# A hybrid decoder layer: every matmul operand starts at a multiple of 128 bytes in SBUF

## The chip, the core and the metric

The kernel runs on one core of one Trainium2 chip. The metric is the device time of one execution in microseconds; the median of three runs is taken. TensorE is written PE (matmuls) and PEld (weight loads), VectorE DVE, ScalarE ACT, GpSimd POOL, SyncE SP.

## What is computed

One decoder layer on a sequence of 256 rows of width 1024, all float32. Cut to what matters here:

```python
h = x @ W_in                                   # split into qA kA vA zA qB kB vB zB gA gB
yA = (swa_sink_attention(qA, kA, vA) * silu(zA)) @ W_oA
yB = (moba_attention(qB, kB, vB) * silu(zB)) @ W_oB
m  = sigmoid(gA + bA) * yA + sigmoid(gB + bB) * yB
x_new = layer_norm(alpha * x + m @ W_out, gamma, beta)
```

## The kernel before

Every large product is made three times, so that float32 accuracy is reached with the type float32r. A weight tile comes by DMA into `raw` (128 x 1024). ACT writes a rounded copy `wh` (line 137, for the last matrix line 134), DVE the rest `wl` = `raw` - `wh` (lines 152 and 149). The activations have such halves too: `xh`, `xl` (the input), `yh`, `yl` (the gated attention), `mh`, `ml` (the merged branches, both in the tile `mm`). A product is then `wh`*`xh` + `wh`*`xl` + `wl`*`xh`.

`contract` (lines 176 to 183) does that for one output tile of 128 columns: lines 180 and 181 alternate over the eight (or four) pieces of the contraction, line 183 follows with `wl`. Each matmul has a new stationary operand, 128 x 128 out of `wh` or `wl`, and a moving operand of 256 columns out of `xh`, `xl`, `yh` or `yl`. There are 37 such tiles of 24 matmuls over the input (`project`), and 16 of 12 matmuls over `yh` and `yl`: 1080 matmuls of 256 columns.

The stages, in order of time: the values (line 292, 320 columns wide, the weights are the moving operand); 21 projections with the attention of eight head pairs among them (scores lines 220 to 222, transposes line 257, values lines 274 and 276); the two gates (16 projections, each followed by 12 matmuls of the output projection of its branch); the last product with `w_out` (line 399), where `mm` is stationary and the weight tiles `wh`, `wl` move.

The last product is done for two row halves. In the first (`t == 0`) two accumulators of 512 columns run together. In the second the columns are taken in three passes: 512 columns, then the third quarter with two columns more (258), then the fourth quarter (256). The two columns more hold the row sums of the fourth quarter of `w_out` (`sums`, put there by POOL in `place_sums`), so that the mean of the whole row is known before the last pass is done, and only the last quarter's normalising is left behind it. For that each of the 16 tiles `wh` and `wl` has four quarters of 258 columns (`OW = 258`).

The order of all instructions is the order of the code; the pools only give addresses. `wh` and `wl` have eight buffers each. A tile of 4 x 258 float32 has 4128 bytes, 32 more than a multiple of 128, so that neighbouring buffers start 32 bytes further round in a line of 128. The small tiles (8, 16 or 32 bytes for a partition) lie among the large ones in the same pools and shift what follows.

Of the kernel before, what the change touches and what calls it, by code (L numbers as in the profile page):

```python
# [11 lines left out]
F32 = mybir.dt.float32  # L12
F32R = mybir.dt.float32r
BF16 = mybir.dt.bfloat16
AF = mybir.ActivationFunctionType
ALU = mybir.AluOpType
# [21 lines left out]
WARM = 9  # L38
RAWS = 5

OW = 258

E = 192

# [2 lines left out]
def hybrid_layer(ctx: ExitStack, tc: tile.TileContext, xT, x2, w_t, w_v, w_a, w_b, w_o,  # L47
# [2 lines left out]
    const = ctx.enter_context(tc.tile_pool(name="const", bufs=1))  # L50
    wp = ctx.enter_context(tc.tile_pool(name="wp", bufs=1))
    work = ctx.enter_context(tc.tile_pool(name="work", bufs=2))
    psum = ctx.enter_context(tc.tile_pool(name="psum", bufs=1, space=bass.MemoryType.PSUM))
    dram = ctx.enter_context(tc.tile_pool(name="dram", bufs=1, space=bass.MemoryType.DRAM))
    ctx.enter_context(tc.manual_schedule())
# [15 lines left out]
    oh = work.tile([NB, RL], F32, tag="res", name="oh")  # L71
    nc.gpsimd.dma_start(tab, table)
    nc.gpsimd.dma_start(oh, onehot)
    sink = const.tile([P, 8], F32, name="sink")
    nc.gpsimd.dma_start(sink, sinks)
    bg = const.tile([P, 16], F32, name="bg")
    nc.gpsimd.dma_start(bg, b_gate)
    ident = const.tile([P, P], F32, name="ident")
    make_identity(nc, ident)
    nsink = const.tile([P, 8], F32, name="nsink")  # L80
    eps = const.tile([P, 1], F32, name="eps")
    nc.gpsimd.memset(eps, LN_EPS)


# [19 lines left out]
    order += [("o", k) for k in range(NK)]  # L104
    ahead = {"v": 2, "t": 3, "a": 4, "b": 5, "o": 7}
    raws, ready = {}, {}
    sums = const.tile([P, NK], F32, name="sums")

    def quarters(w):
        return w.rearrange("p (a b) -> p a b", a=4)[:, :, :S]  # L110

    def fetch(kind, n):

        if kind == "r":

            for a in (2 * n, 2 * n + 1):
                src = bass.AP(tensor=rd.tensor, offset=rd.offset + (a // 8) * 16 * RW + (a % 8) * RL,
                              ap=[[RW + 8, 16], [1, 8], [1, S]])
                nc.sync.dma_start(toep[:, a, :], src)  # L119
            return  # L120
        if kind == "v":
            nc.sync.dma_start(xraw[:, n, :], xT[:, n, :])
            nc.scalar.activation(xh[:, n, :], xraw[:, n, :], AF.Copy)
        width = 640 if kind == "v" else 1024
        src = {"v": lambda: w_v[:, n, :], "t": lambda: w_t[n], "a": lambda: w_a[n], "b": lambda: w_b[n],
               "o": lambda: w_o[n * P:(n + 1) * P, :]}[kind]()
        raw = wp.tile([P, 1024], F32, tag="raw", name="wraw", bufs=RAWS)
        wh = wp.tile([P, 4 * OW], F32R, tag="wh", name="wh", bufs=8)
        parts = 2 if (kind, n) == ("v", 0) else 1
        cuts = [slice(i * width // parts, (i + 1) * width // parts) for i in range(parts)]  # L130
        for cut in cuts:
            nc.sync.dma_start(raw[:, cut], src[:, cut])  # L132
        if kind == "o":
            nc.scalar.activation(quarters(wh), raw.rearrange("p (a b) -> p a b", a=4), AF.Copy)  # L134
        else:
            for cut in cuts:
                nc.scalar.activation(wh[:, cut], raw[:, cut], AF.Copy)  # L137
        raws[kind, n] = raw, wh, width

    def split(kind, n):  # L140

        if kind == "r":
            return
        if kind == "v":
            nc.vector.tensor_sub(xl[:, n, :], xraw[:, n, :], xh[:, n, :].bitcast(F32))
        raw, wh, width = raws.pop((kind, n))
        wl = wp.tile([P, 4 * OW], F32R, tag="wl", name="wl", bufs=8)
        if kind == "o":
            nc.vector.tensor_sub(quarters(wl), raw.rearrange("p (a b) -> p a b", a=4), quarters(wh).bitcast(F32))  # L149
            nc.vector.tensor_reduce(sums[:, n:n + 1], raw[:, 3 * S:], axis=mybir.AxisListType.X, op=ALU.add)  # L150
        else:
            nc.vector.tensor_sub(wl[:, :width], raw[:, :width], wh[:, :width].bitcast(F32))  # L152
        ready[kind, n] = wh, wl

    cursors = [0, 0]
# [16 lines left out]
    def weights(kind, n):  # L172
        lead(kind, n)
        return ready[kind, n]
# [33 lines left out]
    def scores(q, b, heads, sinks_at):  # L208
# [1 line left out]
        qh, ql = q  # L210
        kh, kl = kbd[b]
        pr = work.tile([P, 2, RL], F32, name="pr_", bufs=4)
        nm = work.tile([P, 4], F32, name="nm", bufs=3)
        sm = work.tile([P, 4], F32, name="sm", bufs=3)
        outs = []
        for blk in range(2):
            n = P * (blk + 1)
# [13 lines left out]
                outs.append((dst, at))  # L231
        es = None
        if sinks_at is not None:
            es = work.tile([P, 4], F32, name="es", bufs=3)
            sk = sink[:, sinks_at:sinks_at + 2].unsqueeze(1).to_broadcast([P, 2, 2])
            nc.vector.tensor_tensor(es.rearrange("p (a b) -> p a b", a=2), nm.rearrange("p (a b) -> p a b", a=2), sk,
                                    op=ALU.add)
            nc.scalar.activation(es, es, AF.Exp)
        return pr, outs, sm, es

    def normalise(pr, outs, sm, es):
        if es is not None:
            nc.vector.tensor_add(sm, sm, es)
        rs = work.tile([P, 4], F32, name="rs")
        nc.vector.reciprocal(rs, sm)
        first = pr[:, :, :P]
        nc.gpsimd.tensor_tensor(first, first, rs[:, :2].unsqueeze(2).to_broadcast([P, 2, P]), op=ALU.mult)
        for dst, at in outs[2:]:
            nc.vector.tensor_scalar_mul(dst, dst, rs[:, at:at + 1])
# [120 lines left out]
    gb = const.tile([P, 2, D], F32, tag="ov8", name="gb")  # L370
    nc.sync.dma_start(gb[:, 0, :], gamma.to_broadcast([P, D]))
    nc.sync.dma_start(gb[:, 1, :], beta.to_broadcast([P, D]))
    sd = work.tile([P, 1], F32, name="sd")
    nc.scalar.activation(sd, eps, AF.Sqrt)

    xs = work.tile([P, 1], F32, name="xs")
    nc.vector.tensor_reduce(xs, xr[:, 1, 3 * S:], axis=mybir.AxisListType.X, op=ALU.add)
    nc.vector.tensor_scalar_mul(xs, xs, -ALPHA / D)

    def place_sums():  # L380

        parts = [work.tile([P, NK], F32R, name=f"sums_{i}", bufs=1) for i in range(2)]
        nc.scalar.activation(parts[0], sums, AF.Copy)  # L383
        nc.vector.tensor_sub(parts[1], sums, parts[0].bitcast(F32))
        for k in range(NK):
            for w, part in zip(ready["o", k], parts):
                nc.gpsimd.tensor_copy(w[:, 2 * OW + S:3 * OW], part[:, k:k + 1].to_broadcast([P, 2]))  # L387

    for t in range(2):
        ts = slice(t * P, (t + 1) * P)  # L390
        res = work.tile([P, D], F32, tag="res", name="res")
        st = work.tile([P, 4, 6], F32, name="st")

        def products(accs):
            for k in range(NK):
                wh, wl = (w.rearrange("p (a b) -> p a b", a=4) for w in weights("o", k))
                for a, w, s0, s1 in ((mh, wh, k == 0, False), (ml, wh, False, False), (mh, wl, False, k == NK - 1)):
                    for acc, q, n, cols in accs:
                        nc.tensor.matmul(acc, a[:, k, ts], w[:, q:q + n, :cols], start=s0, stop=s1)  # L399
            if t == 0:  # L400
                place_sums()
            for acc, q, n, _ in accs:
                cut = slice(q * S, (q + n) * S)
                nc.vector.scalar_tensor_tensor(res[:, cut], xr[:, t, cut], ALPHA, acc[:, :n * S], op0=ALU.mult, op1=ALU.add)
                for i in range(q, q + n):
                    nc.vector.bn_stats(st[:, i, :], res[:, i * S:(i + 1) * S])

        def centre(cut, below):
            nc.vector.scalar_tensor_tensor(res[:, cut], res[:, cut], below, gb[:, 0, cut], op0=ALU.add, op1=ALU.mult)
# [3 lines left out]
            nc.gpsimd.tensor_tensor(res[:, early], res[:, early], gb[:, 0, early], op=ALU.mult)  # L413

        early = slice(0, E)
        mv = work.tile([P, 2], F32, name="mv")
        below = work.tile([P, 1], F32, name="below")
        sd = work.tile([P, 1], F32, name="sd")
        rstd = work.tile([P, 1], F32, name="rstd")
        if t == 0:  # L420
            products([(bank("acc"), 0, 2, S), (bank("acc"), 2, 2, S)])
            nc.vector.bn_aggr(mv, st)
            nc.scalar.activation(sd, mv[:, 1:2], AF.Sqrt, bias=eps)
            nc.vector.tensor_scalar_mul(below, mv[:, 0:1], -1.0)
            centre_early(below)
            centre(slice(E, D), below)
        else:
            products([(bank("sc"), 0, 2, S)])
            acc = bank("sc")[:, :OW]
            products([(acc, 2, 1, OW)])  # L430

            part = work.tile([P, 2], F32, name="part")
            nc.vector.bn_aggr(part, st[:, :3, :])
            nc.vector.scalar_tensor_tensor(below, acc[:, S:S + 1], -1.0 / D, xs, op0=ALU.mult, op1=ALU.add)
            nc.vector.scalar_tensor_tensor(below, part[:, 0:1], -0.75, below, op0=ALU.mult, op1=ALU.add)
            centre_early(below)
            centre(slice(E, 3 * S), below)
            products([(bank("pt")[:, :S], 3, 1, S)])
            nc.vector.bn_aggr(mv, st)
            nc.scalar.activation(sd, mv[:, 1:2], AF.Sqrt, bias=eps)  # L440
            centre(slice(3 * S, D), below)
        nc.vector.reciprocal(rstd, sd)

        nc.scalar.activation(res[:, early], res[:, early], AF.Copy, scale=rstd)
# [76 lines left out]
```

## Time and profile before

| | us |
|---|---|
| median of 3 runs | 201.25 |
| lowest, highest | 200.58, 202.72 |
| the profiled execution | 200.9 |
| its span, first to last instruction | 199.1 |

The profiled execution's own time is 1.8 us over its span. The profile gives a matmul's start as measured, its end as modelled; a matmul's row is longer than its share of PE's time, since matmuls overlap. What one costs in a stream is therefore read from start to start here, or from the chain of waits, whose rows hold no overlap.

### The profile page before, as it was taken

To read this page: it belongs to the slowest core of one execution; us is meant where nothing else is said; L and a number is where in the kernel's file an instruction comes from. 1 tells how busy PE (TensorE), PEld (TensorE's weight loads), DVE (VectorE), ACT (ScalarE), POOL (GpSimd) and SP (SyncE) were. 2 spreads that over 40 slices of the span, in tenths; PEclk is the share of its full clock that TensorE was granted. 3 is DMA by queue.
4 is the path that set the end of the run, shared out by engine and by line. 5 is a ranking of instruction groups with operands and counts; after the bars stand their busy time and mean duration, and the time that the engine had idled before them with its cause. 6 is when DMAs were issued, how large, how long until landed. Compare 5 with 4: busy or idle time off the path is not lost.

```text
span 199.1 us, 3871 instructions
## 1 busy us (share of the span) xinstructions
PE 190.9 (96%) x1469; PEld 179.2 (90%) x1469; DVE 137.9 (69%) x280; ACT 114.5 (58%) x228; POOL 19.0 (10%) x45
## 2 busy tenths in 40 slices
PE   8999999999999999999999999999999999999960
PEld 2899999899998998999999999999999999888960
DVE  0686368999987875586768537446585878786773
ACT  5585658677985776765679454246554746630110
POOL 7160000110110101100000000000000000012311
PEclk9999999999999999999999999999999999999995
DMA  5999999947354333044656774573847499300202
GB/s 143 314 402 343 256 298 302 284 137 237 135 163 156 107 105 110 0 154 165 209 185 239 288 243 137 182 216 135 291 145 249 166 304 359 148 0 0 105 0 105
DMA packets 14081, 37.42 MB, mean 188 GB/s; under 512 B 1632, under 2 KB 5744, under 8 KB 14064
## 3 DMA queue, kind: packets, MB, share of 16 engines
q1 hardware_dynamic: 13520, 36.51, 56.2%
q0 software_dynamic: 256, 0.49, 0.7%
q8 instruction: 11, 0.18, 0.3%
q10 hardware_dynamic: 288, 0.20, 0.3%
q14 instruction: 6, 0.05, 0.1%
HBM read 35.75 MB, written 1.44 MB: 187 GB/s over the span
## 4 chain that ended last, share of the span: by engine, by line
PE 77%; DMA 9%; SPq 4%; DVE 3%; ACT 2%; issue 1%; DVEq 0%; ACTq 0%
PE ps_acc L180 19%; PE ps_acc L181 19%; PE ps_acc L183 19%; PE ps_acc L399 6%; PE ps_sc L399 4%; DMA wraw<-in_w_t 4%; PE ps_pt L257 3%; DMA rd<-rvec 3%; DMA wraw<-in_w_v 3%; PE ps_o L274 2%; SPq L119 2%; SPq L132 1%; PE ps_pt L399 1%; PE ps_sc L220 1%; ACT wh L137 1%; PE ps_sc L221 1%
## 5 line engine op out<-in xcount | busy, mean ns | idle before, releaser
L180 PE MATMUL ps_acc<-xh,wh 128*128 128x256 f32 x296 | 71.6, 281 | 0.0
L181 PE MATMUL ps_acc<-xl,wh 128*128 128x256 f32 x296 | 71.3, 280 | 0.0
L152 DVE TENSOR_TENSOR wl<-wraw,wh 128x1024 fp32r<-128x1024 f32 (+1 forms) x53 | 60.7, 1161 | 5.7 <-ACT wh L137 5.4
L137 ACT ACTIVATE wh<-wraw 128x1024 fp32r<-128x1024 f32 (+2 forms) x54 | 52.8, 991 | 8.6 <-DMA wraw<-in_w_t 5.2
L180 PEld LDWEIGHTS ps_acc<-xh,wh 128*128 128x128 f32 x296 | 55.8, 189 | 0.5 <-issue 0.2
L181 PEld LDWEIGHTS ps_acc<-xl,wh 128*128 128x128 f32 x296 | 55.7, 188 | 0.4
L183 PE MATMUL ps_acc<-xh,wl 128*128 128x256 f32 x296 | 40.9, 280 | 0.0
L183 PEld LDWEIGHTS ps_acc<-xh,wl 128*128 128x128 f32 x296 | 37.5, 188 | 0.0
L354 ACT ACTIVATE sg<-ps_acc,bg 128x256 f32<-128x256 f32 x16 | 7.6, 476 | 19.3 <-PE ps_acc L183 19.2
L180 PE MATMUL ps_acc<-yh,wh 128*128 128x256 f32 x64 | 15.8, 281 | 0.0
L181 PE MATMUL ps_acc<-yl,wh 128*128 128x256 f32 x64 | 15.8, 280 | 0.0
L359 DVE TENSOR_TENSOR ga<-ps_acc,sg 128x256 f32<-128x256 f32 x8 | 3.4, 425 | 13.9 <-ACT wh L137 13.9
L180 PEld LDWEIGHTS ps_acc<-yh,wh 128*128 128x128 f32 x64 | 12.1, 188 | 0.0
L181 PEld LDWEIGHTS ps_acc<-yl,wh 128*128 128x128 f32 x64 | 12.0, 188 | 0.0
L387 POOL CAST wh<-sums 128x2 fp32r<-128x2 f32 x8 | 1.5, 187 | 93.8 <-ACT sums L383 93.8
L183 PE MATMUL ps_acc<-yh,wl 128*128 128x256 f32 x64 | 10.1, 279 | 0.0
L364 ACT ACTIVATE mm<-m 128x256 fp32r<-128x256 f32 x8 | 3.4, 419 | 11.6 <-DVE m L363 11.6
L149 DVE TENSOR_TENSOR wl<-wraw,wh 128x1024 fp32r<-128x1024 f32 x8 | 9.8, 1220 | 0.1
L399 PE MATMUL ps_acc<-wh,mm 128*128 128x512 f32 x32 | 8.8, 396 | 0.0
L183 PEld LDWEIGHTS ps_acc<-yh,wl 128*128 128x128 f32 x64 | 8.6, 188 | 0.0
L134 ACT ACTIVATE wh<-wraw 128x1024 fp32r<-128x1024 f32 x8 | 8.2, 1049 | 0.0
L399 PE MATMUL ps_sc<-wh,mm 128*128 128x512 f32 (+1 forms) x32 | 7.9, 339 | 0.0
(162 smaller groups left out, 288.0 us busy)
## 6 DMA issues: line engine op xcount, KB each, us to landing
wraw<-in_w_t SPq DMA_DIRECT2D x37, 512.0 KB, 3.6
wraw<-in_w_o SPq DMA_DIRECT2D x8, 512.0 KB, 5.1
wraw<-in_w_v SPq DMA_DIRECT2D x7, 320.0 KB, 5.4
toep<-rd SPq DMA_DIRECT2D x16, 128.0 KB, 7.1
wraw<-in_w_a SPq DMA_DIRECT2D x4, 512.0 KB, 3.6
wraw<-in_w_b SPq DMA_DIRECT2D x4, 512.0 KB, 3.9
xraw<-in_xT SPq DMA_DIRECT2D x8, 128.0 KB, 5.2
xr<-in_x SPq DMA_DIRECT2D x1, 1024.0 KB, 7.8
```

The costliest lines, as they stand in the source:

```text
L119: nc.sync.dma_start(toep[:, a, :], src)
L134: nc.scalar.activation(quarters(wh), raw.rearrange("p (a b) -> p a b", a=4), AF.Copy)
L137: nc.scalar.activation(wh[:, cut], raw[:, cut], AF.Copy)
L149: nc.vector.tensor_sub(quarters(wl), raw.rearrange("p (a b) -> p a b", a=4), quarters(wh).bitcast(F32))
L152: nc.vector.tensor_sub(wl[:, :width], raw[:, :width], wh[:, :width].bitcast(F32))
L180: nc.tensor.matmul(acc, wh[:, cols[k]], ah[:, a0 + k, :], start=(k == 0), stop=False)
L181: nc.tensor.matmul(acc, wh[:, cols[k]], al[:, a0 + k, :], start=False, stop=False)
L183: nc.tensor.matmul(acc, wl[:, cols[k]], ah[:, a0 + k, :], start=False, stop=(k == n - 1))
L257: nc.tensor.transpose(pt[:, b * P:(b + 1) * P], pr[:, j, b * P:(b + 1) * P], ident)
L274: nc.tensor.matmul(o[r, :], vv[:, 0, c], pts[:, :S], start=True, stop=False)
L354: nc.scalar.activation(sg, acc, AF.Sigmoid, bias=bg[:, at:at + 1])
L399: nc.tensor.matmul(acc, a[:, k, ts], w[:, q:q + n, :cols], start=s0, stop=s1)
```

## The change

The tiles that are smaller than a line of 128 bytes go to a pool of their own, `small`, which is opened after the three others and lies behind them. `OW` becomes 1056: a weight tile is one row of 1056 columns, 4224 bytes, 33 times 128. The quarters are no longer apart. The two columns of sums stand behind the fourth quarter (columns 1024 and 1025); they hold the row sums of the third quarter now, the second pass of the second row half takes the fourth quarter and the two columns (`[3 * S : D + 2]`), and the last pass takes the third quarter. Everything that went by quarters (`quarters`, the reshaped weights, the statistics' order) is adapted to it. Since the columns that are normalised early are now two pieces, one DVE instruction of 576 columns becomes two, of 320 and of 256.

Where the tiles start, in bytes of a partition modulo 128, as the built programs place them:

| tile | before | after |
|---|---|---|
| `xh`, `xl`, `xraw`, `kall`, `pts` | 32 | 0 |
| `yh`, `yl`, `mm`, `vv`, `qh`, `ql`, `pr_`, `raw` | 64 | 0 |
| `ident` | 96 | 0 |
| `wh`, eight buffers by address | 64, 96, 0, 32, 64, 96, 0, 32 | 0 |
| `wl`, eight buffers by address | 64, 96, 0, 32, 64, 96, 0, 32 | 0 |
| third, fourth quarter inside `wh`, `wl` | +16, +24 | +0, +0 |

The pieces of 128 columns inside a weight tile are 512 bytes apart, those of `xh` and its kin 1024 bytes, so that a matmul's two operands keep, before and after, the remainders of their tiles.

```diff
-OW = 258
+OW = 1056
...
+    small = ctx.enter_context(tc.tile_pool(name="small", bufs=2))
...
-    sink = const.tile([P, 8], F32, name="sink")
+    sink = small.tile([P, 8], F32, bufs=1, name="sink")
...
-        wh = wp.tile([P, 4 * OW], F32R, tag="wh", name="wh", bufs=8)
+        wh = wp.tile([P, OW], F32R, tag="wh", name="wh", bufs=8)
...
-        if kind == "o":
-            nc.scalar.activation(quarters(wh), raw.rearrange("p (a b) -> p a b", a=4), AF.Copy)
-        else:
-            for cut in cuts:
-                nc.scalar.activation(wh[:, cut], raw[:, cut], AF.Copy)
+        for cut in cuts:
+            nc.scalar.activation(wh[:, cut], raw[:, cut], AF.Copy)
...
-            nc.vector.tensor_reduce(sums[:, n:n + 1], raw[:, 3 * S:], axis=mybir.AxisListType.X, op=ALU.add)
+            nc.vector.tensor_reduce(sums[:, n:n + 1], raw[:, 2 * S:3 * S], axis=mybir.AxisListType.X, op=ALU.add)
...
-                nc.gpsimd.tensor_copy(w[:, 2 * OW + S:3 * OW], part[:, k:k + 1].to_broadcast([P, 2]))
+                nc.gpsimd.tensor_copy(w[:, D:D + 2], part[:, k:k + 1].to_broadcast([P, 2]))
...
-                    for acc, q, n, cols in accs:
-                        nc.tensor.matmul(acc, a[:, k, ts], w[:, q:q + n, :cols], start=s0, stop=s1)
+                    for acc, lo, hi in accs:
+                        nc.tensor.matmul(acc, a[:, k, ts], w[:, lo:hi], start=s0, stop=s1)
...
-            acc = bank("sc")[:, :OW]
-            products([(acc, 2, 1, OW)])
+            acc = bank("sc")[:, :S + 2]
+            products([(acc, 3 * S, D + 2)])
...
-            centre(slice(E, 3 * S), below)
-            products([(bank("pt")[:, :S], 3, 1, S)])
+            for cut in (slice(E, 2 * S), slice(3 * S, D)):
+                centre(cut, below)
+            products([(bank("pt")[:, :S], 2 * S, 3 * S)])
```

On DVE, at the end of the second row half, between the statistics of the early columns and those of the last pass (`ps_pt`), there stands before:

```order
L435 SCALAR_TENSOR_TENSOR below<-part,below 128x1
L409 SCALAR_TENSOR_TENSOR res<-res,below,gb 128x576
L404 SCALAR_TENSOR_TENSOR res<-xr,ps_pt 128x256
L406 BN_STATS st<-res 128x6
L439 BN_AGGR mv<-st 128x2
L409 SCALAR_TENSOR_TENSOR res<-res,below,gb 128x256
```

And after:

```order
L429 SCALAR_TENSOR_TENSOR below<-part,below 128x1
L403 SCALAR_TENSOR_TENSOR res<-res,below,gb 128x320
L403 SCALAR_TENSOR_TENSOR res<-res,below,gb 128x256
L398 SCALAR_TENSOR_TENSOR res<-xr,ps_pt 128x256
L400 BN_STATS st<-res 128x6
L434 BN_AGGR mv<-st 128x2
L403 SCALAR_TENSOR_TENSOR res<-res,below,gb 128x256
```

The 576 columns are two instructions now; nothing else has moved on DVE. On ACT, where the last rounded copies of `w_out` stand behind those of the merged branches (`mm`), there stands before:

```order
L134 ACTIVATE wh<-wraw 128x4x256
L354 ACTIVATE sg<-ps_acc,bg 128x256
L364 ACTIVATE mm<-m 128x256
L374 ACT_TABLE_LOAD
L374 ACTIVATE sd<-eps 128x1
L134 ACTIVATE wh<-wraw 128x4x256 x3
L383 ACTIVATE sums_2366<-sums 128x8
```

And after:

```order
L132 ACTIVATE wh<-wraw 128x1024
L347 ACTIVATE sg<-ps_acc,bg 128x256
L357 ACTIVATE mm<-m 128x256
L367 ACT_TABLE_LOAD
L367 ACTIVATE sd<-eps 128x1
L132 ACTIVATE wh<-wraw 128x1024 x3
L376 ACTIVATE sums_2369<-sums 128x8
```

The copies stand in the same places, without the gaps between quarters. On PE, POOL and SP each instruction of before has its counterpart in the same place, with the same waits; there the change is one of addresses alone.

## Rows read from the trace of the kernel before

**Rows 1.** The page: span, busy time, PE and its granted clock in 40 slices.

```profile
span 199.1 us, 3871 instructions
...
PE 190.9 (96%) x1469; PEld 179.2 (90%) x1469; DVE 137.9 (69%) x280; ACT 114.5 (58%) x228; POOL 19.0 (10%) x45
...
PEclk9999999999999999999999999999999999999995
```

**Rows 2.** The chain that ended last: start us, us, what; where it joins PE.

```profile
35.28 0.97 DVE pr__420 L249 x2
...
38.09 0.47 PE ps_sc L220
```

**Rows 3.** Busy time in two stretches, all engines.

```profile
20.00:28.00 8.00, 8.00 (x69) 8.00 (x68) 4.03 (x6) 4.59 (x9) 0.00 (x0) 1.00 1.07 260
...
100.00:140.00 40.00, 40.00 (x343) 40.00 (x343) 24.19 (x29) 22.75 (x30) 0.00 (x0) 1.00 0.62 208
```

**Rows 4.** Timeline of PE: first matmuls of the gates, and of the last product.

```profile
101.89 0.28 PE L180 MATMUL ps_acc<-xh,wh 128*128 128x256 f32 x1
...
169.64 0.62 PE L399 MATMUL ps_acc<-wh,mm 128*128 128x512 f32 x2
```

**Rows 5.** Timeline of PE: first matmul of some projections and of what follows.

```profile
23.14 0.28 PE L180 MATMUL ps_acc<-xh,wh 128*128 128x256 f32 x1
...
26.02 0.28 PE L180 MATMUL ps_acc<-xh,wh 128*128 128x256 f32 x1
...
28.83 0.28 PE L220 MATMUL ps_sc<-kall,qh 128*128 128x256 f32 x1
...
96.39 0.28 PE L180 MATMUL ps_acc<-xh,wh 128*128 128x256 f32 x1
...
99.13 0.28 PE L180 MATMUL ps_acc<-xh,wh 128*128 128x256 f32 x1
```

**Rows 6.** The chain again: eight matmuls of line 183 (`wl` stationary) in a stream.

```profile
43.75 0.95 PE ps_acc L183 x8
...
49.28 0.96 PE ps_acc L183 x8
...
57.63 0.96 PE ps_acc L183 x8
60.46 0.93 PE ps_acc L183 x8
65.95 0.94 PE ps_acc L183 x8
...
79.76 0.95 PE ps_acc L183 x8
...
92.79 0.96 PE ps_acc L183 x8
95.62 0.94 PE ps_acc L183 x8
98.39 0.91 PE ps_acc L183 x8
```

**Rows 7.** Timeline of PE: the three passes of the last product, second row half.

```profile
183.67 0.63 PE L399 MATMUL ps_sc<-wh,mm 128*128 128x512 f32 x2
...
186.47 0.40 PE L399 MATMUL ps_sc<-wh,mm 128*128 128x258 f32 x2
...
189.35 0.40 PE L399 MATMUL ps_pt<-wh,mm 128*128 128x256 f32 x2
...
191.86 0.40 PE L399 MATMUL ps_pt<-wh,mm 128*128 128x256 f32 x2
```

**Rows 8.** Timeline of DVE at the end: early columns, last pass.

```profile
190.94 0.82 DVE L409 SCALAR_TENSOR_TENSOR res<-res,below,gb 128x576 f32<-128x576 f32 x1
...
192.41 0.42 DVE L404 SCALAR_TENSOR_TENSOR res<-xr,ps_pt 128x256 f32<-128x256 f32 x1 [0.65 <-PE ps_pt L399]
...
193.51 0.42 DVE L409 SCALAR_TENSOR_TENSOR res<-res,below,gb 128x256 f32<-128x256 f32 x1
```

More of the change, by code (lines that the diff above doesn't have):

```diff
@@ L73, in hybrid_layer @@
     nc.gpsimd.dma_start(oh, onehot)
-    sink = const.tile([P, 8], F32, name="sink")
+    sink = small.tile([P, 8], F32, bufs=1, name="sink")
     nc.gpsimd.dma_start(sink, sinks)
-    bg = const.tile([P, 16], F32, name="bg")
+    bg = small.tile([P, 16], F32, bufs=1, name="bg")
     nc.gpsimd.dma_start(bg, b_gate)
@@ L79, in hybrid_layer @@
     make_identity(nc, ident)
-    nsink = const.tile([P, 8], F32, name="nsink")
-    eps = const.tile([P, 1], F32, name="eps")
+    nsink = small.tile([P, 8], F32, bufs=1, name="nsink")
+    eps = small.tile([P, 1], F32, bufs=1, name="eps")
     nc.gpsimd.memset(eps, LN_EPS)
@@ L106, in hybrid_layer @@
     raws, ready = {}, {}
-    sums = const.tile([P, NK], F32, name="sums")
-    def quarters(w):
-        return w.rearrange("p (a b) -> p a b", a=4)[:, :, :S]
+    sums = small.tile([P, NK], F32, bufs=1, name="sums")
     def fetch(kind, n):
@@ L146, in split @@
         raw, wh, width = raws.pop((kind, n))
-        wl = wp.tile([P, 4 * OW], F32R, tag="wl", name="wl", bufs=8)
+        wl = wp.tile([P, OW], F32R, tag="wl", name="wl", bufs=8)
+        nc.vector.tensor_sub(wl[:, :width], raw[:, :width], wh[:, :width].bitcast(F32))
         if kind == "o":
-            nc.vector.tensor_sub(quarters(wl), raw.rearrange("p (a b) -> p a b", a=4), quarters(wh).bitcast(F32))
-            nc.vector.tensor_reduce(sums[:, n:n + 1], raw[:, 3 * S:], axis=mybir.AxisListType.X, op=ALU.add)
-        else:
-            nc.vector.tensor_sub(wl[:, :width], raw[:, :width], wh[:, :width].bitcast(F32))
+            nc.vector.tensor_reduce(sums[:, n:n + 1], raw[:, 2 * S:3 * S], axis=mybir.AxisListType.X, op=ALU.add)
         ready[kind, n] = wh, wl
@@ L212, in scores @@
         pr = work.tile([P, 2, RL], F32, name="pr_", bufs=4)
-        nm = work.tile([P, 4], F32, name="nm", bufs=3)
-        sm = work.tile([P, 4], F32, name="sm", bufs=3)
+        nm = small.tile([P, 4], F32, name="nm", bufs=3)
+        sm = small.tile([P, 4], F32, name="sm", bufs=3)
         outs = []
@@ L233, in scores @@
         if sinks_at is not None:
-            es = work.tile([P, 4], F32, name="es", bufs=3)
+            es = small.tile([P, 4], F32, name="es", bufs=3)
             sk = sink[:, sinks_at:sinks_at + 2].unsqueeze(1).to_broadcast([P, 2, 2])
@@ L243, in normalise @@
             nc.vector.tensor_add(sm, sm, es)
-        rs = work.tile([P, 4], F32, name="rs")
+        rs = small.tile([P, 4], F32, name="rs")
         nc.vector.reciprocal(rs, sm)
@@ L372, in hybrid_layer @@
     nc.sync.dma_start(gb[:, 1, :], beta.to_broadcast([P, D]))
-    sd = work.tile([P, 1], F32, name="sd")
+    sd = small.tile([P, 1], F32, name="sd")
     nc.scalar.activation(sd, eps, AF.Sqrt)
-    xs = work.tile([P, 1], F32, name="xs")
-    nc.vector.tensor_reduce(xs, xr[:, 1, 3 * S:], axis=mybir.AxisListType.X, op=ALU.add)
+    xs = small.tile([P, 1], F32, name="xs")
+    nc.vector.tensor_reduce(xs, xr[:, 1, 2 * S:3 * S], axis=mybir.AxisListType.X, op=ALU.add)
     nc.vector.tensor_scalar_mul(xs, xs, -ALPHA / D)
     def place_sums():
-        parts = [work.tile([P, NK], F32R, name=f"sums_{i}", bufs=1) for i in range(2)]
+        parts = [small.tile([P, NK], F32R, name=f"sums_{i}", bufs=1) for i in range(2)]
         nc.scalar.activation(parts[0], sums, AF.Copy)
@@ L391, in hybrid_layer @@
         res = work.tile([P, D], F32, tag="res", name="res")
-        st = work.tile([P, 4, 6], F32, name="st")
+        st = small.tile([P, 4, 6], F32, name="st")
         def products(accs):
             for k in range(NK):
-                wh, wl = (w.rearrange("p (a b) -> p a b", a=4) for w in weights("o", k))
+                wh, wl = weights("o", k)
                 for a, w, s0, s1 in ((mh, wh, k == 0, False), (ml, wh, False, False), (mh, wl, False, k == NK - 1)):
-                    for acc, q, n, cols in accs:
-                        nc.tensor.matmul(acc, a[:, k, ts], w[:, q:q + n, :cols], start=s0, stop=s1)
+                    for acc, lo, hi in accs:
+                        nc.tensor.matmul(acc, a[:, k, ts], w[:, lo:hi], start=s0, stop=s1)
             if t == 0:
                 place_sums()
[L402 to L406, printed above, removed]
+            for acc, lo, hi in accs:
+                n = min(hi, D) - lo
+                cut = slice(lo, lo + n)
+                nc.vector.scalar_tensor_tensor(res[:, cut], xr[:, t, cut], ALPHA, acc[:, :n], op0=ALU.mult, op1=ALU.add)
+                for at in range(lo, lo + n, S):
+                    nc.vector.bn_stats(st[:, (0, 1, 3, 2)[at // S], :], res[:, at:at + S])
         def centre(cut, below):
@@ L415, in hybrid_layer @@
         early = slice(0, E)
[L416 to L419, printed above, removed]
+        mv = small.tile([P, 2], F32, name="mv")
+        below = small.tile([P, 1], F32, name="below")
+        sd = small.tile([P, 1], F32, name="sd")
+        rstd = small.tile([P, 1], F32, name="rstd")
         if t == 0:
-            products([(bank("acc"), 0, 2, S), (bank("acc"), 2, 2, S)])
+            products([(bank("acc"), 0, 2 * S), (bank("acc"), 2 * S, D)])
             nc.vector.bn_aggr(mv, st)
@@ L427, in hybrid_layer @@
         else:
-            products([(bank("sc"), 0, 2, S)])
-            acc = bank("sc")[:, :OW]
-            products([(acc, 2, 1, OW)])
-            part = work.tile([P, 2], F32, name="part")
+            products([(bank("sc"), 0, 2 * S)])
+            acc = bank("sc")[:, :S + 2]
+            products([(acc, 3 * S, D + 2)])
+            part = small.tile([P, 2], F32, name="part")
             nc.vector.bn_aggr(part, st[:, :3, :])
@@ L436, in hybrid_layer @@
             centre_early(below)
-            centre(slice(E, 3 * S), below)
-            products([(bank("pt")[:, :S], 3, 1, S)])
+            for cut in (slice(E, 2 * S), slice(3 * S, D)):
+                centre(cut, below)
+            products([(bank("pt")[:, :S], 2 * S, 3 * S)])
             nc.vector.bn_aggr(mv, st)
             nc.scalar.activation(sd, mv[:, 1:2], AF.Sqrt, bias=eps)
-            centre(slice(3 * S, D), below)
+            centre(slice(2 * S, 3 * S), below)
         nc.vector.reciprocal(rstd, sd)
```

## The prediction

> **What bounds the kernel now.** I read the page first: PE is busy for 190.9 of 199.1 us, at the full granted clock until the last slice [rows 1]. Then the chain of waits: it hangs on transfers, ACT and DVE up to 38.09 us, and from there on PE to the last matmul [rows 2]. Then the stretches: in the gates (100 to 140 us) PE is busy for all of 40.00 us, DVE for 24.19, ACT for 22.75, the DMA engines for 0.62 of their time; between 20 and 28 us the DMA engines are full (1.07) [rows 3]. So what a matmul costs from start to start is what the kernel costs, from 38 us to 192 us, and the engines beside PE have room for a somewhat faster or slower one.
>
> The change leaves the order of PE, POOL and SP as it is. It moves addresses, so the question is what an address does to a matmul. The profile doesn't print addresses; the built program has them, and the trace has the starts.
>
> **What one matmul costs.** From the first matmul of the gates to the first of the last product lie 16 x (24 + 12) = 576 matmuls of 256 columns and nothing else: 169.64 - 101.89 = 67.75 us, 117.6 ns each [rows 4]. At the upper clock level of 2.4 GHz, a column per clock would be 256 / 2.4 = 106.7 ns. So there are some 11 ns in each that are neither columns nor a lower clock, and this is all that an address could give back.
>
> The 117.6 ns is a mean of different rhythms. Whole projections of 24 matmuls: 26.02 - 23.14 = 2.88 us, 120.0 ns each; 28.83 - 26.02 = 2.81 us, 117.1 ns; 99.13 - 96.39 = 2.74 us, 114.2 ns [rows 5]. The work is the same; what differs is the buffer of `wh` and `wl`, so the addresses. I took the weight buffers from the built program in the order of their use and put each stream beside its **distance**: the moving operand's start minus the stationary one's, modulo 128. The three projections have distances of 0, 32 and 64. The eight matmuls of line 183 show it again [rows 6]:
> - distance 0 (rows at 43.75, 57.63, 79.76, 92.79): 0.95, 0.96, 0.95, 0.96 us, mean 0.955, so 119.4 ns each;
> - distance 32 (60.46, 95.62): 0.93 and 0.94, so 116 to 118 ns;
> - distance 64 (65.95, 98.39): 0.94 and 0.91; the second and the first of these use the same buffers, so the rhythm is not a matter of the address alone; 114 to 118 ns;
> - distance 96 (49.28): 0.96, 120 ns.
>
> Is it the distance, or each operand's own place in a line of 128 bytes? For the moving operand there is a test: in the second row half of the last product `mm` stays at 64 while the moving weights start anywhere. The pass of 512 columns starts at multiples of 32, 0 and 64 among them: 24 matmuls, of which the last 12 take 186.47 - 183.67 = 2.80 us, 233.3 ns. The pass of 258 columns starts at odd multiples of 16: 24 matmuls in 189.35 - 186.47 = 2.88 us, 120.0 ns. The pass of 256 columns starts at 24, 56, 88 or 120: 21 in 191.86 - 189.35 = 2.51 us, 119.5 ns [rows 7]. The three passes cost 0.456, 0.465 and 0.467 ns a column: a start 8 bytes off a multiple of 16 costs nothing that shows against one at a multiple of 16, and the starts at a multiple of 128 don't stand out. For the stationary one, the projection of 117.1 ns has both weight buffers at 0 modulo 128 and is slower than that of 114.2 ns, whose buffers are at 96. So no operand gains by being at a multiple of 128 by itself, as far as these rows go. What no row shows is both at 0 at once: `xh`, `xl` are at 32 before, `yh`, `yl` and `mm` at 64.
>
> **The change part by part.**
> - *The aligned operands.* With everything at 0 the distance is 0 in every matmul. The nearest rows are those of distance 0, where both operands are at 32: 119.4 ns. They even cover the finer remainders: modulo 512 the distances after are 0, 128, 256 and 384, and the buffers at distance 0 before have 0, 128, 256 and 384 as well. Against the mean of 117.6 ns this is 1.8 ns more. From 38 us on there are 1080 - 5 x 24 = 960 matmuls of 256 columns; the first five projections (120) lie where transfers and DVE end last [rows 2, 3]. 960 x 1.8 ns = 1.7 us. The bounds: the fastest stream, 0.91 / 8 = 113.8 ns, gives 960 x (113.8 - 117.6) = -3.6 us; the slowest, 120.0 ns, +2.3 us. I take the value of distance 0, as its rows differ from the changed kernel in the least. The passes of 512 columns I leave at 233.3 ns (distances of 0 and 64 are among them): 0, between -0.5 and +0.5 us for 72 of them if they moved as the others do.
> - *The last product's passes.* The third and the fourth quarter change places; the columns and the matmuls are as many: 0.
> - *One more DVE instruction.* 576 columns take 0.82 us and 256 take 0.42, so 320 take by the same slope 0.42 + 64 x 0.40 / 320 = 0.50; the pair 0.92, 0.10 us more. It ends at some 191.9 us, and DVE then waited 0.65 us for PE's last pass [rows 8]: 0. Were that cover gone, 0.1 us.
> - *Copies of the last matrix without gaps; small tiles in a pool behind.* The same elements on ACT and DVE, which have room beside PE [rows 3]: 0. The transfers land 64 or 32 bytes earlier in a line; where they bind, before 38 us, the DMA engines are full at any address of before (1.07), so 0, with a few tenths either way.
>
> The sum against the profiled execution: 200.9 + 1.7 = **202.6 us**. The median of the runs is 0.35 us above that execution; on it the sum would be 202.95.
>
> **The skill against the rows.** The Trainium skill ("TensorE: Matmul & The Clock Gate", "Step-by-step: what each phase is for") says that PE has two independent SBUF read ports, one for the moving operand and one for weight loads, so that loading the next weights takes nothing from the running matmul. By that rule the distance would mean nothing, the 1.7 us would fall away and the sum would be 200.9. The rows of equal work at 114.2 and 120.0 ns [rows 5] speak against it as a full account, though they don't say through what the two operands meet.
>
> **The rivals.**
> - *The alignment takes the 11 ns away.* For it: no row has both operands at 0, so it isn't excluded, and the whole of the 11 ns is unexplained. Against it: it would have to need both at once, as neither alone shows anything, and the surplus grows with the columns (20 ns at 512, 11 at 256), as an effect of a start would not. Price: 960 x (106.7 - 117.6) = -10.5 us, 72 x (213.3 - 233.3) = -1.4 us, 48 x -13 ns = -0.6 us, so 188.4 us. The Trainium skill (same page, "Back-to-back issue gap") gives N / 2.4 + 2.5 ns for matmuls in a row, 109.2 ns at 256 columns; with that the time would be about 191, an estimate, and no run here shows it.
> - *The fast rhythm locks everywhere.* The same buffers run at 0.94 and at 0.91 us [rows 6], so a rhythm depends on how a stream begins too; with one address pattern throughout, the streams could all fall into the fast one. Price -3.6 us: 197.3. Against it: four rows at distance 0, none under 0.95.
> - *Slower than the measurement can miss.* With distance 0 throughout, each stream hands the slow rhythm of 120.0 ns, seen in the first of rows 5, to the next one, and the broad passes take their share: 200.9 + 2.3 + 0.5 = 203.7, or 204 on the median. It decides from a mean of about 119.7 ns for the 960 (201.25 + 1% = 203.3).
> - *Nothing changes*: the rhythms are an accident of how streams begin, and their mean stays at 117.6 ns. 200.9 to 201.3.
>
> **How the numbers follow.** A difference of 1% of the median, 2 us, is about what a measurement of this kernel can tell from no change. The forecast (about 202 to 203.2) has 0.40, the slower one 0.23, nothing changes 0.10, the fast rhythm 0.18 (of which a part comes out less than 1% faster), the full gain 0.09. So faster by over 1%: 0.26; within: 0.50; slower: 0.24. The range leaves out the full gain and the far ends of the others: 197.0 to 204.6.
>
> **What would show it.** In the profile after, all rows of eight matmuls of line 183's successor at 0.95 or 0.96 us and the 576 matmuls of the gates in 68.8 us (119.4 ns) would bear me out. The step that I am least sure of is that both at 0 behaves as both at 32. If the gates take 65.5 us, the fast rhythm has won; at 62 us the alignment does all that it could. The passes of 512 columns should stay at 233 ns; if they fall too, the cause is not in the weight loads, since there is one for each matmul whatever its width. DVE should still wait for the last pass at the end. A difference that lies before 38 us would mean the transfers, which I hold to be untouched.

## The result, and the profile after

The changed kernel takes 202.5 us (median of 20 runs, 201.76 to 202.78), the kernel before 201.22 us beside it (20 runs): a ratio of 1.0052, 95% interval 1.0031 to 1.0073. It is slower, by half a per cent. The profiled execution after took 202.46 us with a span of 200.7, against 200.9 and 199.1 before.

The page after, the same lines as in [rows 1]:

```profile
span 200.7 us, 3872 instructions
...
PE 192.2 (96%) x1469; PEld 180.8 (90%) x1469; DVE 137.8 (69%) x281; ACT 114.3 (57%) x228; POOL 19.1 (10%) x45
...
PEclk9999999999999999999999999999999999999998
```

One instruction more on DVE, 1.3 us more on PE, the granted clock as before. The timeline of PE after has these first rows of the projections behind 38 us, of the gates and of the last product; the second and third answer to [rows 4]:

```profile
39.16 0.28 PE L173 MATMUL ps_acc<-xh,wh 128*128 128x256 f32 x1
...
102.74 0.28 PE L173 MATMUL ps_acc<-xh,wh 128*128 128x256 f32 x1
...
171.39 0.86 PE L392 MATMUL ps_acc<-wh,mm 128*128 128x512 f32 x3
...
188.00 0.41 PE L392 MATMUL ps_sc<-wh,mm 128*128 128x258 f32 x2
```

In the kernel before, the row that answers to the first one is this:

```profile
38.85 0.28 PE L180 MATMUL ps_acc<-xh,wh 128*128 128x256 f32 x1
```

The 576 matmuls from the gates' first row to the last product's take 171.39 - 102.74 = 68.65 us, 119.2 ns each, against 67.75 us and 117.6 ns before: 0.90 us of the loss. The gates begin 0.85 us later than before (102.74 against 101.89). Of that, 0.54 us lie among the attention (102.74 - 39.16 = 63.58 us against 101.89 - 38.85 = 63.04; PE is busy for all of both), where 384 matmuls of 256 columns stand, so about 1.4 ns each. The other 0.31 us lie ahead of it (39.16 against 38.85), where the transfers bind; that part differs between the profiled executions (the first projection begins at 20.31 us before, 20.98 after, 20.16 in `mix` and 24.15 in `d64q`), and one execution of each can't tell whether the change has a share in it. The 72 matmuls of 512 columns take 188.00 - 171.39 = 16.61 us, 230.7 ns each; before they took 186.47 - 169.64 = 16.83 us, 233.8 ns [rows 4, 7]: 0.22 us came back there. 0.85 + 0.90 - 0.22 is 1.53 of the 1.56 us.

The chain of waits after, rows of eight matmuls with `wl` stationary (line 176 now), which answer to [rows 6]:

```profile
58.02 0.96 PE ps_acc L176 x8
...
66.44 0.96 PE ps_acc L176 x8
...
96.24 0.96 PE ps_acc L176 x8
99.10 0.95 PE ps_acc L176 x8
101.95 0.96 PE ps_acc L176 x8
104.82 0.94 PE ps_acc L176 x8
...
109.11 0.96 PE ps_acc L176 x8
```

Before they went from 0.91 to 0.96, by the buffers; now each buffer gives 0.94 to 0.96. So one distance still leaves small differences between buffers. At the end DVE after, which answers to [rows 8]:

```profile
192.50 0.95 DVE L403 SCALAR_TENSOR_TENSOR res<-res,below,gb 128x320 f32<-128x320 f32 x2
193.95 0.42 DVE L398 SCALAR_TENSOR_TENSOR res<-xr,ps_pt 128x256 f32<-128x256 f32 x1 [0.50 <-PE ps_pt L392]
```

The two instructions (of 320 and 256 columns) take 0.95 us together instead of 0.82, and DVE still waits 0.50 us for PE's last pass.

### The profile page after: what moved, and what is told of

Same layout as the page of the kernel before. It is cut to its first block, busy times and chain, and to the rows that moved or that the text cites. A ratio compares the mean times of both kernels' runs of the same rounds, so it can differ in the third digit from the quotient of the medians.

```text
span 200.7 us, 3872 instructions
## 1 busy us (share of the span) xinstructions
PE 192.2 (96%) x1469; PEld 180.8 (90%) x1469; DVE 137.8 (69%) x281; ACT 114.3 (57%) x228; POOL 19.1 (10%) x45
## 3 DMA queue, kind: packets, MB, share of 16 engines
HBM read 35.75 MB, written 1.44 MB: 185 GB/s over the span
## 4 chain that ended last, share of the span: by engine, by line
PE 92%; DMA 3%; DVE 1%; SPq 1%; ACT 1%; DVEq 0%; issue 0%; ACTq 0%
PE ps_acc L173 21%; PE ps_acc L174 21%; PE ps_acc L176 21%; PE ps_acc L392 6%; PE ps_sc L392 4%; PE ps_acc L285 3%; PE ps_pt L250 3%; PE ps_sc L285 3%; DMA wraw<-in_w_v 3%; PE ps_o L267 2%; PE ps_pt L392 1%; PE ps_sc L213 1%; PE ps_sc L214 1%; PE ps_sc L215 1%; PE ps_o L269 1%; DVEq L512 0%
## 5 line engine op out<-in xcount | busy, mean ns | idle before, releaser
L143 DVE TENSOR_TENSOR wl<-wraw,wh 128x1024 fp32r<-128x1024 f32 (+1 forms) x61 | 70.5, 1168 | 6.6 <-ACT wh L132 6.4
L173 PE MATMUL ps_acc<-xh,wh 128*128 128x256 f32 x296 | 72.6, 283 | 0.0
L174 PE MATMUL ps_acc<-xl,wh 128*128 128x256 f32 x296 | 72.4, 283 | 0.0
L132 ACT ACTIVATE wh<-wraw 128x1024 fp32r<-128x1024 f32 (+2 forms) x62 | 60.8, 995 | 7.7 <-DMA wraw<-in_w_t 3.9
L174 PEld LDWEIGHTS ps_acc<-xl,wh 128*128 128x128 f32 x296 | 56.3, 190 | 0.3
L176 PEld LDWEIGHTS ps_acc<-xh,wl 128*128 128x128 f32 x296 | 38.0, 190 | 0.0
L191 DVE TENSOR_TENSOR kall<-ps_acc,kall 64x256 fp32r<-64x256 f32 x10 | 4.2, 421 | 4.5 <-ACT kall L189 4.4
L392 PEld LDWEIGHTS ps_acc<-wh,mm 128*128 128x128 f32 x32 | 5.9, 188 | 1.3
```

The source lines that it names most:

```text
L173: nc.tensor.matmul(acc, wh[:, cols[k]], ah[:, a0 + k, :], start=(k == 0), stop=False)
L174: nc.tensor.matmul(acc, wh[:, cols[k]], al[:, a0 + k, :], start=False, stop=False)
L176: nc.tensor.matmul(acc, wl[:, cols[k]], ah[:, a0 + k, :], start=False, stop=(k == n - 1))
L191: nc.vector.tensor_sub(l[r, j, :], acc[r, :], h[r, j, :].bitcast(F32))
L392: nc.tensor.matmul(acc, a[:, k, ts], w[:, lo:hi], start=s0, stop=s1)
```

## The experiments

Each kernel is the changed kernel with the edit shown; the ratio is to the kernel before, measured beside it. The distance is the moving operand's start minus the stationary one's, modulo 128. The last column is worked out as above, from the first matmul of the gates to the first of the last product; it is a mean over matmuls, and those of one distance are not all alike.

| run | distance, activations moving | median us, or one time | ratio to before | 576 matmuls: us, ns each |
|---|---|---|---|---|
| before | scattered | 201.22 | 1 | 67.75, 117.6 |
| changed | 0 | 202.5 | 1.0052 (1.0031 to 1.0073) | 68.65, 119.2 |
| `all32` | 0, all at 32 | 202.61 | 1.0072 (1.0054 to 1.009) | 68.65, 119.2 |
| `d96` | 96 | 202.13 | 1.0043 (1.0006 to 1.0081) | 68.55, 119.0 |
| `scatter` | scattered | 201.2 | 1.0011 (0.9987 to 1.0034) | 67.96, 118.0 |
| `d48` | 48 | 201.14 | 0.9986 (0.9958 to 1.0013) | 67.83, 117.8 |
| `d32` | 32 | 200.35 | 0.9975 (0.9956 to 0.9994) | 67.58, 117.3 |
| `mix` | 64 and 0 | 199.1 | one run | 66.98, 116.3 |
| `d64` | 64 | 197.52 | 0.9827 (0.9809 to 0.9845) | 65.28, 113.3 |
| `d64q` | 64, scores too | 197.41 | 0.9818 (0.978 to 0.9857) | 65.28, 113.3 |

**Distance 64** (`d64`):

```diff
 OW = 1056
+OFF = 16
...
-        wh = wp.tile([P, OW], F32R, tag="wh", name="wh", bufs=8)
+        wh = wp.tile([P, OW], F32R, tag="wh", name="wh", bufs=8)[:, OFF:OFF + D + 2]
...
-        wl = wp.tile([P, OW], F32R, tag="wl", name="wl", bufs=8)
+        wl = wp.tile([P, OW], F32R, tag="wl", name="wl", bufs=8)[:, OFF:OFF + D + 2]
```

> The changed kernel, with every wh and wl tile begun 64 bytes further on in its buffer; all else still at a multiple of 128, so that the distance (moving start minus stationary start, modulo 128) is 64 everywhere. Theory of the distance: matmuls of 256 columns at 113.4 to 118 ns, mean about 116 as at distance 64 before; against 119.3 in the changed kernel that is 960 x 3.3 ns = 3.2 us less than it, so about 199.3 us, ratio to the kernel before about 0.990. Rival, each operand's own place: half of the operands leave the multiple of 128, so the mean goes at most half of the way back to 117.7 ns, about 0.8 us less than the changed kernel, ratio 1.001. Rival, the other edits (pool, passes, split DVE step) cost the time: unchanged, ratio 1.005.

It came out faster than the theory of the distance said: 197.52 us, ratio 0.9827, 5 us under the changed kernel and below the kernel before. The first row of the gates and the first of the last product:

```profile
101.18 0.28 PE L174 MATMUL ps_acc<-xh,wh 128*128 128x256 f32 x1
...
166.46 0.85 PE L393 MATMUL ps_acc<-wh,mm 128*128 128x512 f32 x3
```

166.46 - 101.18 = 65.28 us, 113.3 ns for each of the 576. The chain of waits of this run, rows of eight with `wl` stationary (line 177):

```profile
28.37 0.91 PE ps_acc L177 x8
...
32.22 0.94 PE ps_acc L177 x8
...
36.10 0.91 PE ps_acc L177 x8
...
40.60 0.94 PE ps_acc L177 x8
...
59.99 0.91 PE ps_acc L177 x8
...
65.44 0.94 PE ps_acc L177 x8
68.27 0.94 PE ps_acc L177 x8
...
92.24 0.94 PE ps_acc L177 x8
95.00 0.91 PE ps_acc L177 x8
97.72 0.91 PE ps_acc L177 x8
...
160.28 0.91 PE ps_acc L177 x8
164.36 0.91 PE ps_acc L177 x8
```

There are two rhythms at one distance: 0.94 us (117.8 ns from start to start) in 12 of the 14 rows from 36.10 to 92.24, 0.91 us (113.3 ns) in all 19 from 95.00 to 164.36. In the kernel before, each change of buffers brought another distance; here, in the unbroken stream from 95 us on, nothing ends the fast rhythm. That is the rest of the gain. Ahead of that it does end: the rows at 28.37, 36.10 and 59.99 are fast, and the next ones (32.22, 40.60, 65.44), behind matmuls of the attention, are slow again. Both rivals fall: a place effect would have given 0.8 us at most, the other edits none.

**All operands at 32, distance 0** (`all32`):

```diff
+    const.tile([P, 8], F32, name="pad")
     tab = const.tile([NB, 2 * P], F32, name="tab")
```

> The changed kernel, with a tile of 32 bytes ahead of all others in the first pool, so that every operand starts at 32 modulo 128 and no distance changes (0 everywhere). Theory of the distance: as the changed kernel, 119.3 ns for a matmul of 256 columns, ratio to the kernel before 1.005. Rival, each operand's own place: at 32 the operands are where half of them were before, so the mean returns to about 117.7 ns and the ratio to about 1.000 or beyond.

202.61 us, and the 576 matmuls of the gates take as long as in the changed kernel, to the hundredth of a microsecond:

```profile
102.97 0.28 PE L174 MATMUL ps_acc<-xh,wh 128*128 128x256 f32 x1
...
171.62 0.39 PE L393 MATMUL ps_acc<-wh,mm 128*128 128x512 f32 x1
```

171.62 - 102.97 = 68.65 us. No operand is at a multiple of 128 any more, and nothing has changed: between 0 and 32, the place of both operands in a line does not matter.

**The other edits with scattered weights** (`scatter`):

```diff
-OW = 1056
+OW = 1032
```

> The changed kernel with weight tiles of 1032 columns instead of 1056 (4128 bytes, as before), so that the buffers start at 0, 32, 64 and 96 in turn and the distances are scattered as before, while the pool of small tiles, the new passes and the split DVE step stay. Theory of the distance: mean back at about 117.7 ns, ratio to the kernel before 1.000 (between 0.997 and 1.002). Rival, the other edits cost the time: ratio stays at 1.005. Rival, each operand's own place: activations still at 0, so a part of the loss stays, 1.002 to 1.004.

201.2 us, ratio 1.0011 (0.9987 to 1.0034): level with the kernel before. The pool of small tiles, the new order of the passes and the split DVE step cost at most 0.3% and nothing that this measurement shows.

**Distances 32, 96 and 48** (`d32`, `d96`, `d48`): as `d64`, with `OFF = 24` in `d32`, `OFF = 8` in `d96` and `OFF = 20` in `d48` (columns of 4 bytes) in place of `OFF = 16`.

> As the run at distance 64, with the weight tiles begun 96 bytes further on: distance 32 for the matmuls with the activations moving, 96 for those with the weights moving. Theory of the distance: mean about 117.4 ns as at distance 32 before, so 960 x 1.9 ns = 1.8 us less than the changed kernel, ratio to the kernel before about 0.997. Rival, each operand's own place: weights at 96 instead of 64, no reason for a difference to the run at distance 64.

> As the run at distance 64, with wh and wl begun 32 bytes further on: distance 96 for the matmuls with the activations moving, 32 for those with the weights moving. Theory of the distance: 118.9 ns as at distance 96 before, so near the changed kernel: 960 x 0.4 ns = 0.4 us less, about 202, ratio 1.003. Rival, the run at distance 64 gained because its weight tiles are not at a multiple of 128: then this one gains as well, ratio 0.985.

> As the run at distance 64, with wh and wl begun 80 bytes further on: distance 48. Asks whether the steps are 32 bytes wide. If the cost follows the distance smoothly, the rhythm lies between those of 32 (117.3 ns) and 64 (113.3 to 117.8, mean 114.7): about 116 ns, 198.5 to 199.5 us. If what counts is a block of 32 bytes, 48 runs as 32: 117.3 ns, 200.3 us, ratio 0.997; or as 64: 197.5 us.

The first rows of the gates and of the last product in `d32`:

```profile
101.29 0.28 PE L174 MATMUL ps_acc<-xh,wh 128*128 128x256 f32 x1
...
168.87 0.39 PE L393 MATMUL ps_acc<-wh,mm 128*128 128x512 f32 x1
```

and in `d96`:

```profile
104.60 0.28 PE L174 MATMUL ps_acc<-xh,wh 128*128 128x256 f32 x1
...
173.15 0.63 PE L393 MATMUL ps_acc<-wh,mm 128*128 128x512 f32 x2
```

Both came as the trace of before had priced these distances: 168.87 - 101.29 = 67.58 us, 117.3 ns, and 173.15 - 104.60 = 68.55 us, 119.0 ns, ratios 0.9975 and 1.0043. In `d96` the weight tiles leave the multiple of 128 just as in `d64`, and nothing is gained, so it isn't that. `d48` was a miss: 117.8 ns, ratio 0.9986. It lies neither between 32 and 64 nor on either of them, though close to 32; the cost doesn't follow the distance smoothly, and whether it goes by blocks of 32 bytes is not told apart by 0.5 ns.

**Two distances in one kernel** (`mix`): `wh` begins 64 bytes further on, `wl` at a multiple of 128.

```diff
 OW = 1056
+OFF_H, OFF_L = 16, 0
...
-        wh = wp.tile([P, OW], F32R, tag="wh", name="wh", bufs=8)
+        wh = wp.tile([P, OW], F32R, tag="wh", name="wh", bufs=8)[:, OFF_H:OFF_H + D + 2]
...
-        wl = wp.tile([P, OW], F32R, tag="wl", name="wl", bufs=8)
+        wl = wp.tile([P, OW], F32R, tag="wl", name="wl", bufs=8)[:, OFF_L:OFF_L + D + 2]
```

> The changed kernel with wh begun 64 bytes further on and wl left at a multiple of 128. Two thirds of the matmuls of a projection (lines 174 and 175, wh stationary) then have distance 64, the last third (line 177, wl) distance 0, in one kernel. Theory of the distance: lines 174 and 175 at 113.4 to 118 ns, line 177 at 119 to 120 ns, in the same tiles; mean about 117, near 200.5 us. Rival: the gain of the run at distance 64 is one of the whole kernel (placement of the program, another clock, transfers), not of the pair of addresses: then both kinds run alike.

The timeline of PE shows both rhythms in one projection:

```profile
109.35 0.28 PE L174 MATMUL ps_acc<-xh,wh 128*128 128x256 f32 x1
109.46 0.28 PE L175 MATMUL ps_acc<-xl,wh 128*128 128x256 f32 x1
...
111.16 1.12 PE L177 MATMUL ps_acc<-xh,wl 128*128 128x256 f32 x8
112.12 0.28 PE L174 MATMUL ps_acc<-yh,wh 128*128 128x256 f32 x1
```

Sixteen matmuls on `wh` in 111.16 - 109.35 = 1.81 us, 113.1 ns each; the eight on `wl` in 112.12 - 111.16 = 0.96 us, 120.0 ns. So the rhythm goes with the pair of tiles, not with the execution. (That `wh` runs before `wl` isn't the reason: in `d64` the rows with `wl` take 0.91 us in the gates.) Its one time, 199.1 us, lies 1.4 below what was expected: many streams on `wh`, like this one, fell into the fast rhythm.

**The scores at distance 64 too** (`d64q`):

```diff
-        qh = work.tile([P, S], F32R, name="qh")
+        qh = work.tile([P, S + 32], F32R, name="qh")[:, OFF:OFF + S]
...
-        ql = work.tile([P, S], F32R, name="ql")
+        ql = work.tile([P, S + 32], F32R, name="ql")[:, OFF:OFF + S]
```

> The run at distance 64 with qh and ql, too, begun 64 bytes further on, so that the scores' matmuls (kall moving, qh or ql stationary) have distance 64. At distance 64 two rhythms were seen, 117.8 and 113.3 ns; the projections among the attention hold the slow one, which they enter from the scores, the gates hold the fast one. If the scores' own distance sets how the next projection begins: those projections fall to 113.4, 14 x 24 x 4.4 ns = 1.5 us less, about 196.1 us, ratio 0.975. Rival, it is the pause or the other kind of matmul ahead that sets the slow rhythm: no change, 197.5 us, ratio 0.983.

197.41 us, ratio 0.9818: not the 0.975 that was expected, and not to be told from `d64`. In the profiled execution the projections begin at 24.15 us, against 20.93 in `d64`, so only what follows is compared: among the attention 9 of 14 rows of eight are at 0.91 us, where `d64` had 2. That points to a part of the scores in how the next projection begins, by one execution of each kernel, and they don't settle it alone. Seven projections more at the fast rhythm would be 7 x 24 x 4.5 ns = 0.8 us, 0.4% of the time, and the interval of this run alone is 0.978 to 0.9857. As to time, the run decides nothing between the two.

**Narrower stationary operands** (`half0`, `quarter0`, `half64`): all but the first two and the last matmul of a tile load 64 (in `quarter0` 32) columns instead of 128 and write as many rows of the sum instead of 128, so that the other rows lack most of theirs. `half64` has `OFF = 16` besides, as `d64`.

```diff
+        part = lambda k, whole: (acc, cols[k]) if whole else (acc[:HD, :], slice(cols[k].start, cols[k].start + HD))
         for k in range(n):
-            nc.tensor.matmul(acc, wh[:, cols[k]], ah[:, a0 + k, :], start=(k == 0), stop=False)
-            nc.tensor.matmul(acc, wh[:, cols[k]], al[:, a0 + k, :], start=False, stop=False)
+            to, c = part(k, k == 0)
+            nc.tensor.matmul(to, wh[:, c], ah[:, a0 + k, :], start=(k == 0), stop=False)
+            nc.tensor.matmul(to, wh[:, c], al[:, a0 + k, :], start=False, stop=False)
         for k in range(n):
-            nc.tensor.matmul(acc, wl[:, cols[k]], ah[:, a0 + k, :], start=False, stop=(k == n - 1))
+            to, c = part(k, k == n - 1)
+            nc.tensor.matmul(to, wl[:, c], ah[:, a0 + k, :], start=False, stop=(k == n - 1))
```

> The changed kernel (distance 0), but in the projections and the branch outputs all matmuls except a tile's first and last have a stationary operand of 64 columns instead of 128: 128 x 64 is loaded, 256 columns still move, and half of the outputs lack most of their sum. It asks what the moving stream meets. If it is the next weight load's reads: with half of them the surplus over 106.7 ns falls, from 13 ns to 6 to 10, so 113 to 117 ns at distance 0. Rival, the surplus lies in the moving stream alone, or in writing the sums: 120 ns stays.

> As the run with stationary operands of 64 columns at distance 0 (mean 115.8 ns against 119.3 with 128), now with 32 columns: 128 x 32 is loaded for 256 moving columns; three quarters of the outputs lack most of their sum. Theory that the moving stream meets the next weight load's reads: the mean falls further, to the fastest rhythm seen, 113.3 ns, and no lower if the rest of the surplus (113.3 - 106.7 = 6.6 ns) belongs to the moving stream itself; towards 108 to 110 if all of the surplus comes from the loads. Rival, the narrow operand itself is what made the run faster, not its reads: stays at 115.8.

> Stationary operands of 64 columns as in the other such run, but with wh and wl begun 64 bytes further on, so at distance 64; half of the outputs lack most of their sum. If 113.3 ns is the moving stream's own pace, which the loads only spoil: 113.3 nearly everywhere, the rhythm of 117.8 ns among the attention gone or rarer, mean 113.3 to 114.5. Rival, the loads are in the 113.3 as well: below 113.

The first rows of the gates, two rows of eight with `wl` stationary out of the chain of waits, and the first row of the last product, in `half0`:

```profile
100.98 0.28 PE L175 MATMUL ps_acc<-xh,wh 128*128 128x256 f32 x1
101.10 0.28 PE L176 MATMUL ps_acc<-xl,wh 128*128 128x256 f32 x1
101.22 0.28 PE L175 MATMUL ps_acc<-xh,wh 128*64 128x256 f32 x1
...
107.16 0.92 PE ps_acc L179 x8
...
111.31 0.92 PE ps_acc L179 x8
...
167.69 0.39 PE L395 MATMUL ps_acc<-wh,mm 128*128 128x512 f32 x1
```

and in `quarter0`:

```profile
100.87 0.28 PE L175 MATMUL ps_acc<-xh,wh 128*128 128x256 f32 x1
...
167.76 0.40 PE L395 MATMUL ps_acc<-wh,mm 128*128 128x512 f32 x1
```

With 64 columns loaded (198.77 us, one run) the 576 matmuls take 167.69 - 100.98 = 66.71 us, 115.8 ns, against 119.2 ns with 128: the same moving streams at the same distance run faster with a narrower stationary operand. That it is the smaller load is argued and not shown, since fewer rows of the sum are written too. Nor is the fast rhythm bound to distance 64: at distance 0, 9 of the 16 rows of eight in the gates of `half0` take 0.92 us (113.3 ns from start to start). With 32 columns (198.83 us, one run) it is 167.76 - 100.87 = 66.89 us, 116.1 ns, not the 113.3 that was expected: the effect is not in proportion to the columns. At distance 64 with 64 columns (197.51 us, one run) the gates take 65.28 us as in `d64`, 113.3 ns, and not less, as the first theory had it; but the slow rhythm among the attention didn't become rarer, which it had also said: 2 of the 14 rows there are at 0.91 us, as many as in `d64`.

## Why the prediction was right

The forecast was 202.6 us for the profiled execution and 202.95 on the median; they came to 202.46 and 202.5. The mechanism held. That the first pair agrees to 0.14 us is in part luck: where 1.7 us were foreseen, the matmuls of 256 columns behind 38 us cost 1.44, the passes of 512 columns gave 0.22 back, and 0.31 us lie ahead of 38 us, where the prediction had nothing but a few tenths either way. By the ratio of the medians the loss is 1.05 us (0.6 to 1.5), so 1.7 was too much.

- *PE sets the time.* Held: the engines beside it are busy as before, and `d64` shows the other side of it, where PE is busy for 4.8 us less (187.4 against 192.2) and the span is 5.0 us shorter (195.7 against 200.7).
- *Alignment by itself is worth nothing; the distance sets the rhythm.* Held, and shown by `all32` (same time with no operand aligned), `d96` (nothing gained by weight tiles off the multiple of 128) and `mix` (two rhythms in one tile). The distance is not all of it: at 64 there are two rhythms, and at 0 the rows go from 0.94 to 0.96 us.
- *Both at 0 behaves as both at 32: 119.4 ns.* This was the least certain step. The gates gave 119.2 ns, 68.65 us where 68.8 was named, and `all32` the same. The rows of eight were to be at 0.95 or 0.96 us throughout; some are at 0.94 (104.82).
- *960 x 1.8 ns = 1.7 us.* By the rows: 0.90 us in the gates, where 576 x 1.8 = 1.04 was foreseen, and 0.54 among the attention, where 384 x 1.8 = 0.7 was. The term is 1.44 us, somewhat too large, with the right sign and cause.
- *The passes of 512 columns at no change.* Off by a little, inside the bounds given: 3.1 ns less for each of 72, 0.22 us. They fell while the gates rose. The prediction had thought of a fall of both, as a sign against the weight loads; this fall doesn't settle that.
- *The split DVE step is hidden.* Held: 0.13 us more on DVE instead of 0.10, inside a wait of which 0.50 us is left.
- *The other edits cost nothing.* Held by `scatter`, within 0.3%.

Of the rivals, the full gain of 11 ns, the fast rhythm at distance 0, the slower one (119.7 ns or more) and an unchanged mean (117.6) did not come; no stream came near the 109.2 ns at which the prediction also priced the first. The fast rhythm, however, is what distance 64 brings: the prediction had put its rows at 114 to 118 ns for 64, but saw in it no more than a rival for the change itself. The Trainium skill's two independent read ports ("TensorE: Matmul & The Clock Gate", "Step-by-step: what each phase is for") can't be the whole account: equal streams ran at 113.1 and 120.0 ns in `mix` by the stationary tile's address, and narrower stationary operands took 3.4 ns off in `half0`.

What stays open: through what the two operands meet; whether the load or the rows written make the narrower operand faster, and why it counts once (128 to 64 columns) and then not (64 to 32); why distance 64 has two rhythms and what makes a stream enter one of them; and where the 6.6 ns between 106.7 and 113.3 ns come from, since no run went below 113.

## What to carry to other kernels

Where PE's matmuls stream without waits (here float32r, 256 columns, a new stationary operand for each), read them from start to start, and compare streams of equal work: 3 to 6% lay between the fastest rhythm (113.3 ns) and the others (117.3 to 120.0) by the addresses of the two operands. Aligning every operand to the same boundary is not neutral; it gives all pairs one relation, here the slowest of the five tried. Shift one family of tiles against the other by 64 bytes instead (`d64`, 197.52 us, 1.7% under the kernel before), and try some other distances, since they cost one constant each.

## What the runs showed of the hardware

- A float32r matmul of 128 x 128 by 256 columns at the full granted clock took from 113.3 (`d64`) to 120.0 ns (`mix`, with `wl`) from start to start in steady streams; no stream came to the 106.7 ns of a column per clock at 2.4 GHz.
- In steady streams its mean pace went by the difference of the two operands' start addresses modulo 128: 0, 119.2 ns; 32, 117.3; 48, 117.8; 64, 113.3 or 117.8; 96, 119.0. Whether all operands start at 0 or at 32 made no difference (68.65 us twice, changed kernel and `all32`).
- The fast rhythm at distance 64 persists in an unbroken stream: 576 matmuls in a row kept 113.3 ns (`d64`). Ahead of that, behind matmuls of the attention, it was lost three times.
- At 512 columns the order is another one: 230.7 ns at distance 0, 233.8 with scattered ones. Distance 64 gave 230.7 as well (`d64`, 183.07 - 166.46 = 16.61 us for 72).
